# Three quarters of the MLPs' and of the second layer's inputs, and eight heads' probabilities, are turned in 32x32 blocks through DRAM instead of on TensorE

## The chip, the cores and the metric

The kernel runs on one core of one Trainium2 chip. The metric is the time of one execution on the device in microseconds. The kernel before took 2045.74 us (median of three runs, 2043.22 to 2048.05). The execution that was profiled took 2041.28 us, of which 2039.5 us are the span from its first to its last instruction.

## The reference

A two-layer encoder on 256 tokens of width 2048, all in float32. Each layer normalizes its input, projects it, runs twelve heads of its own kind and four heads into a memory of 256 tokens, projects the heads' outputs back (`w_o`), and runs an MLP with a squared ReLU. Layer 0's heads see a neighbourhood with a bias, layer 1's are grouped-query heads with normalized and rotated queries and keys.

```python
for i in range(DEPTH):
    n = rms_norm(h, attn_norm[i])
    ...
    h = h + jnp.concatenate([mix, cross], axis=-1) @ w_o[i]
    n = rms_norm(h, mlp_norm[i])
    h = h + jnp.square(jax.nn.relu(n @ w_up[i])) @ w_down[i]
return rms_norm(h, final_norm)
```

and a head of either kind is

```python
s = jnp.einsum(..., q, k) * scale (+ bias)
p = jax.nn.softmax(s, axis=-1)
return jnp.einsum(..., p, v)
```

## The kernel before, in words

**Products.** Every float32 operand is split in two parts of lower precision, `hi` and `lo` (`split`, L304: ScalarE copies to `hi`, VectorE subtracts for `lo`), and a product is three matmuls: hi by hi, hi by lo, lo by hi. Weights come from DRAM in chunks of 1 MB (`raw`, three buffers, loaded on SyncE's queue) and are split in halves; four pairs of halves are in hand. A half of an ordinary chunk is 12 matmuls of 512 columns.

**Turning.** The residual `h` lies with tokens on partitions. A projection needs its input with features on partitions, so it has to be turned: `transposed` (L318) has TensorE transpose 128x128 pieces into PSUM (`pt_n`), and `split_pair` (L329) takes them from there, times the norm's gain, into the two parts of `hT` (an MLP's input) or `nT` (a layer's input). The 2048 features are four column blocks of 512; a block is 8 transposes and 4 split pairs. A head's probabilities `sc` are turned too before they meet the values: by four transposes into `pt_a` (`attend2`, L406), or, in layer 0's twelve own heads, by the other way that the kernel has: VectorE transposes 32x32 blocks within their partitions (`turned`, L390), and `moved` (L352) puts the blocks in their places by writing them to DRAM in four pieces on SyncE's queue (`turn`) and reading them back in one on GpSimd's. `attend2_turned` then splits from there.

**Order.** `run_all` walks a list of grains (half chunks). A grain is a tick. `later(n, fn)` runs `fn` n ticks on, and loads and splits are written some grains ahead of their matmuls. A scheduler then orders each engine's instructions; on the chip each engine and each queue runs its own in order.

**Output projection and MLP input** (`o_done`, L646). When a column block `nb` of the projection is done, it is added to `h` and its squares are summed. The MLP's norm is one factor per token. Since a squared ReLU only scales, any positive factor will do for the input, if the result is corrected (`inv`, L671). Before, the factor came from the first three blocks (`guard`, ticks after the third), and only then were these three scaled (`scaled`) and transposed. The last block is prepared in `begun`, finished from PSUM and transposed on TensorE.

**Layer 1's input.** `down_done` (L986) closes a block of layer 0's MLP and has it transposed one tick later.

**Attention.** `attention` (L430) spreads a head's three steps (scores and softmax; turn; values) over ticks, `blocks` giving the distances for heads turned through DRAM. Layer 1's heads come four at a time (`b_q_done`, L1103), each four behind a block of queries.

Of the kernel before, what the change touches and what calls it, by code (L numbers as in the profile page):

```python
# [17 lines left out]
P = 128  # L18
D = 2048
# [20 lines left out]
GUARD = 3  # L40
# [38 lines left out]
def encoder_kernel(ctx: ExitStack, tc: tile.TileContext, t: dict, out: bass.AP):  # L79
# [70 lines left out]
    def halves_of(w):  # L150
# [9 lines left out]
        def prep(hf):  # L160
            if hf == 0:
                tiles["raw"] = at.ring.tile([P, CH], F32, tag="raw", bufs=3, name="raw")
                nc.sync.dma_start(tiles["raw"], w.src)
            tiles[hf] = new_half(w.kind)
            split(*tiles[hf], tiles["raw"][:, hf * HALF : (hf + 1) * HALF])
# [393 lines left out]
    def x_stats():  # L559
        ss = small.tile([P, NT], F32, tag="ss0", name="x_ss")  # L560
        for i in range(NT):
            for b in range(4):
                sq = at.work.tile([P, 512], F32, tag="b_y2", name="sq")
                nc.scalar.activation(sq, h[:, i, b * 512 : (b + 1) * 512], AF.Square, accum_out=ssq[0][:, i, b : b + 1])
        nc.vector.tensor_reduce(ss, ssq[0], axis=AX.X, op=ALU.add)
        box["x_col"] = keep.tile([P, NT], F32, name="x_col")
        nc.vector.tensor_copy(box["x_col"], rstd_of(ss, D, "x"))
        box["x_row"] = at.work.tile([P, SEQ], F32, tag="x_row", bufs=1, name="x_row")
        along_free(box["x_col"], box["x_row"])
# [75 lines left out]

    def o_done(layer, nb):  # L646
        which = 2 * layer

        def guard():

            box["near"] = mean_square(which, GUARD, "near")
            box["scale"] = keep.tile([P, NT], F32, tag="scale", name="scale")
            nc.gpsimd.tensor_tensor(box["scale"], box["near"], mhalf[:, :NT], op=ALU.pow)
            box["hT"] = wide(f"hT{layer}")

        def begun():

            y = at.side.tile([P, NT, 512], F32, tag="T", bufs=2, name="h_s")
            for i in range(NT):
                nc.scalar.activation(y[:, i, :], h[:, i, D - 512 :], AF.Copy, scale=box["scale"][:, i : i + 1])  # L660
            box["begun"] = y

        def scaled(b):
            y = at.side.tile([P, NT, 512], F32, tag="T", bufs=2, name="h_s")
# [3 lines left out]
            transposed(box["hT"], lambda i, k: y[:, i, k % 4 * P : (k % 4 + 1) * P],  # L668
                       list(range(b * 4, b * 4 + 4)), (G_M0, G_M1)[layer])
# [10 lines left out]
        def f(w):  # L680
            if nb == 0:
                closed("work")
                at.side = opened("side", side="right")
            def add():
# [8 lines left out]
            if nb < 3:  # L693
                add()
                squares()
            if nb == GUARD - 1:
                later(1, guard)
                for b in range(GUARD):
                    later(2 + 2 * b, scaled, b)
                later(7, begun)  # L700
# [210 lines left out]
    def plain_grains(layer, nb):  # L911
# [9 lines left out]
        def prep(c, hf):  # L921
            if c == 0:
                own[c, hf] = half_of_side(own[0], hf, PLAIN_AT)
            else:
                own[c, hf] = tuple(at.mlp.tile([P, HALF], F32R, tag="bt"[hf] + x, name=f"{x}_p") for x in "hl")
                split(*own[c, hf], own[1][:, hf * HALF : (hf + 1) * HALF])
# [58 lines left out]

    def down_done(layer, nb):  # L986
        def f(w):
# [7 lines left out]
            if nb == 0:  # L995
                box["nT"] = wide("nT1", 480)
            later(1, transposed, box["nT"], lambda i, k: h[:, i, k * P : (k + 1) * P],
                  list(range(nb * 4, nb * 4 + 4)), G_A1)
            if nb == 3:
# [3 lines left out]
                def norm():  # L1003
                    box["rstd"] = keep.tile([P, NT], F32, name="rstd1")
                    v = mean_square(1, 4, "full")
                    nc.gpsimd.tensor_tensor(box["rstd"], v, mhalf[:, :NT], op=ALU.pow)
# [96 lines left out]
    def b_q_done(blk):  # L1103
        def f(w):
# [5 lines left out]
                       for j, kv in enumerate(kvs)], 1, 2, 3)  # L1110
# [20 lines left out]
    def to_work():  # L1131
        closed("side")
        open_work(3)
# [144 lines left out]
```

## Time and profile before

| | before |
|---|---|
| median of the runs, us | 2045.74 (2043.22 to 2048.05) |
| the profiled execution, us | 2041.28 |
| its span, us | 2039.5 |
| VectorE, ScalarE, GpSimd, busy share of the span | 82%, 61%, 6% |
| DMA, mean over the span | 216 GB/s |
| weight chunks of 1 MB for the MLPs' first half | 128, 6.4 us from issue to landing |

In the groups below a row has the source line, the engine, the operation, what it writes and reads, the shapes and the count; then the busy time in us, the mean of one in ns, and the idle time of its engine just before with what ended it. Rows of the timeline have start and length in us first. Rows of windows have the stretch, its length and each engine's busy time with its number of instructions (TensorE's matmuls, its weight loads, VectorE, ScalarE, GpSimd), then TensorE's granted clock, the DMA share and GB/s. Rows of waits have the total, the number and the longest.

### The profile page before, as it was taken

The numbers are of one execution on the slowest core, as the hardware profiler recorded it, in microseconds if no ns is written. First come the engines' busy times: TensorE is split into PE (matmuls) and PEld (weight loads), VectorE is DVE, ScalarE is ACT, GpSimd is POOL, SyncE is SP. The second block draws the span as 40 slices with busy tenths as digits, with TensorE's granted clock in tenths as the row PEclk, the third lists the DMA queues.
The fourth block names the chain that finished last, engine by engine and source line by source line (L and its number), as shares of the span: only waits on it lengthen the run. The fifth ranks groups of instructions, "written<-read, shape, count | busy, mean of one in ns | idle before, by whom it ended". The sixth has DMA issues, their size and how long they took to land.

```text
span 2039.5 us, 32742 instructions
## 1 busy us (share of the span) xinstructions
PE 2018.9 (99%) x13044; PEld 1827.2 (90%) x13044; DVE 1665.5 (82%) x2049; ACT 1241.9 (61%) x1628; POOL 125.3 (6%) x156
## 2 busy tenths in 40 slices
PE   8999999999999999999999999999999999999998
PEld 7899999889999999999988888889999999999986
DVE  6767677558989999989997667657999999999896
ACT  6655455456666666666656557556666666666654
POOL 0000000000000000010000001000000000000000
PEclk9999999999999999999999999999999999999999
DMA  7756666727778787777765454537777787777773
GB/s 281 276 200 202 218 211 213 287 83 239 231 220 240 222 239 229 224 236 232 229 207 220 176 170 145 199 113 235 236 230 231 222 239 228 231 224 230 230 220 137
DMA packets 101306, 440.16 MB, mean 216 GB/s; under 512 B 11424, under 2 KB 19232, under 8 KB 68000
## 3 DMA queue, kind: packets, MB, share of 16 engines
q1 hardware_dynamic: 82800, 402.40, 58.4%
q0 software_dynamic: 17776, 34.61, 9.1%
q8 instruction: 102, 1.67, 0.3%
q10 hardware_dynamic: 576, 1.05, 0.1%
q14 instruction: 52, 0.43, 0.1%
HBM read 401.32 MB, written 7.34 MB: 200 GB/s over the span
## 4 chain that ended last, share of the span: by engine, by line
PE 95%; DVE 2%; DMA 1%; issue 1%; ACT 1%; SPq 0%; POOLq 0%; POOL 0%; DVEq 0%; ACTq 0%
PE ps_u L742 11%; PE ps_u L740 11%; PE ps_u L741 11%; PE p L859 9%; PE p L858 9%; PE p L857 8%; PE ps_m L214 8%; PE ps_m L217 8%; PE ps_m L218 8%; PE ps_s L226 3%; PE ps_s L228 3%; PE ps_s L227 3%; DVE ul L307 1%; DMA raw<-in_w_km 1%; PE pt_n L324 1%
## 5 line engine op out<-in xcount | busy, mean ns | idle before, releaser
L742 PE MATMUL ps_u<-hT,ul 128*128 128x256 f32 x2048 | 567.1, 277 | 2.3 <-DVE ul L307 2.3
L740 PE MATMUL ps_u<-hT,uh 128*128 128x256 f32 x2048 | 565.6, 276 | 0.1
L741 PE MATMUL ps_u<-hT,uh 128*128 128x256 f32 x2048 | 565.6, 276 | 0.0
L306 ACT ACTIVATE uh<-raw_U 128x1024 fp32r<-128x1024 f32 x278 | 294.6, 1060 | 306.6 <-PE ps_u L741 280.2
L740 PEld LDWEIGHTS ps_u<-hT,uh 128*128 128x128 f32 x2048 | 384.5, 188 | 5.7 <-ACT uh L306 0.5
L741 PEld LDWEIGHTS ps_u<-hT,uh 128*128 128x128 f32 x2048 | 384.3, 188 | 5.4
L742 PEld LDWEIGHTS ps_u<-hT,ul 128*128 128x128 f32 x2048 | 384.4, 188 | 4.5 <-DVE ul L307 3.5
L307 DVE TENSOR_TENSOR lo<-raw,hi 128x1024 fp32r<-128x1024 f32 (+1 forms) x224 | 266.1, 1194 | 148.8 <-ACT hi L306 147.4
L307 DVE TENSOR_TENSOR ul<-raw_U,uh 128x1024 fp32r<-128x1024 f32 x278 | 337.2, 1218 | 38.9 <-ACT uh L306 38.8
L306 ACT ACTIVATE hi<-raw 128x1024 fp32r<-128x1024 f32 (+1 forms) x224 | 231.5, 1039 | 205.4 <-PE ps_m L218 112.2
L306 ACT ACTIVATE th<-t 128x2048 fp32r<-128x2048 f32 x112 | 215.1, 1921 | 124.4 <-PE p L859 116.1
L307 DVE TENSOR_TENSOR tl<-t,th 128x2048 fp32r<-128x2048 f32 x112 | 256.1, 2287 | 29.9 <-ACT th L306 29.4
L307 DVE TENSOR_TENSOR bl<-b,bh 128x1536 fp32r<-128x1536 f32 x112 | 196.0, 1750 | 0.3
L858 PE MATMUL p<-tl,a_s 128*128 128x512 f32 x448 | 176.1, 393 | 0.3 <-DVE tl L307 0.3
L859 PE MATMUL p<-th,a_s 128*128 128x512 f32 x448 | 176.3, 394 | 0.0
L306 ACT ACTIVATE bh<-b 128x1536 fp32r<-128x1536 f32 x112 | 166.2, 1484 | 7.7 <-PE p L859 1.3
L837 POOL DMA_DIRECT2D t<-b x112 | 96.4, 860 | 1157.1 <-DVE t L836 551.8
L857 PE MATMUL p<-th,a_s 128*128 128x512 f32 x448 | 163.6, 390 | 0.0
L859 PE MATMUL p<-bh,a_s 128*128 128x512 f32 x336 | 131.7, 392 | 0.0
L858 PE MATMUL p<-bl,a_s 128*128 128x512 f32 x336 | 131.0, 390 | 0.0
L228 PE MATMUL ps_s<-nT,lo 128*128 128x256 f32 x448 | 125.4, 280 | 0.0
L226 PE MATMUL ps_s<-nT,hi 128*128 128x256 f32 x448 | 125.2, 279 | 0.0
(237 smaller groups left out, 3770.2 us busy)
## 6 DMA issues: line engine op xcount, KB each, us to landing
raw_U<-in_w_up SPq DMA_DIRECT2D x128, 1024.0 KB, 6.4
b<-in_w_pair SPq DMA_DIRECT2D x112, 768.0 KB, 4.5
raw<-in_w_o SPq DMA_DIRECT2D x32, 1024.0 KB, 5.0
t<-in_w_pair SPq DMA_DIRECT2D x112, 256.0 KB, 3.4
t<-b POOLq DMA_DIRECT2D x112, 256.0 KB, 6.7
raw<-in_w_b SPq DMA_DIRECT2D x21, 1024.0 KB, 5.0
raw<-in_w_av SPq DMA_DIRECT2D x12, 1024.0 KB, 5.0
raw<-in_w_aq SPq DMA_DIRECT2D x12, 1024.0 KB, 4.9
```

The source lines that it names most:

```text
L214: first = nc.tensor.matmul(w.ps[i], ah, hi[:, s], start=st, stop=False)
L217: nc.tensor.matmul(w.ps[i], ah, lo[:, s], start=False, stop=False)
L226: nc.tensor.matmul(ps, hi[:, s], acts[:, k, :SEQ], start=k == 0, stop=False)
L228: nc.tensor.matmul(ps, lo[:, s], acts[:, k, :SEQ], start=False, stop=k == KT - 1)
L306: first = nc.scalar.activation(dst_hi, src, AF.Copy)
L307: return first, nc.vector.tensor_tensor(dst_lo, src, dst_hi.bitcast(F32), op=ALU.subtract)
L740: nc.tensor.matmul(ps, hi[:, s], acts[:, k, :SEQ], start=k == 0, stop=False)
L741: nc.tensor.matmul(ps, hi[:, s], acts[:, k, SEQ:], start=False, stop=False)
L742: nc.tensor.matmul(ps, lo[:, s], acts[:, k, :SEQ], start=False, stop=k == KT - 1)
L857: nc.tensor.matmul(ps, a[:, 0, ai, :], hi[:, s], start=begins, stop=False)
L858: nc.tensor.matmul(ps, a[:, 0, ai, :], lo[:, s], start=False, stop=False)
L859: nc.tensor.matmul(ps, a[:, 1, ai, :], hi[:, s], start=False, stop=ends)
```

## The change

Two new functions carry it. `turned_rows` turns a column block as `turned` turns a head: 32x32 blocks on VectorE, then `moved`. `landed` splits what came back, times the gain, from SBUF: four ScalarE instructions and eight smaller VectorE ones for a block. `landed_past` places it behind the last weight split written so far.

- Both MLPs' inputs: the factor is now one known before the projection (layer 0: `x_col` of the kernel's input, layer 1: `rstd` of its own input), with its mean square kept for `inv`. So blocks 0 to 2 are scaled and turned each as it is done (`turning`), landing 6, 6 and 5 ticks later. Block 3 stays on TensorE.
- Layer 1's input: blocks 0 to 2 go the same way (`turned_input`), block 3 stays.
- Layer 1's first eight heads use `blocks=(0, 6, 8)`; the last four and the memory heads stay. The buffers for scores go from 3 to 7, and GpSimd's descriptor space in SBUF is set to 8192 bytes.

```diff
+    def turned_rows(src, room, back):
+        nc.vector.transpose(room.rearrange("p (b k i j) -> p i k b j", b=4, k=4, i=2),
+                            src.rearrange("p i (k b r) -> p i k b r", k=4, b=4))
+        back = back.rearrange("p (a f) -> p a f", a=4)
+        moved(back, room.rearrange("p (b f) -> p b f", b=4))
+        return back
+
+    def landed(dst, back, b, which):
+        src = back.rearrange("p a (k i j) -> p k i a j", k=4, i=2)
+        for k in range(4):
+            n, g = b * 4 + k, gain(which, b * 4 + k)
+            hi, lo = (dst[:, n, x * SEQ : (x + 1) * SEQ].rearrange("p (i a j) -> p i a j", i=2, a=4) for x in range(2))
+            nc.scalar.activation(hi, src[:, k], AF.Copy, scale=g)
+            for i in range(NT):
+                nc.vector.scalar_tensor_tensor(lo[:, i], src[:, k, i], g, hi[:, i].bitcast(F32),
+                                               op0=ALU.mult, op1=ALU.subtract)
+
+    def landed_past(*args):
+        past(lambda: landed(*args), box["splits"][-1])
...
-        def guard():
-            box["near"] = mean_square(which, GUARD, "near")
-            box["scale"] = keep.tile([P, NT], F32, tag="scale", name="scale")
-            nc.gpsimd.tensor_tensor(box["scale"], box["near"], mhalf[:, :NT], op=ALU.pow)
+        def factors():
+            box["scale"] = box[("x_col", "rstd")[layer]]
+            box["near"] = box[("x_mean", "mean")[layer]]
             box["hT"] = wide(f"hT{layer}")
...
+        def turning():
+            y = at.side.tile([P, 2, NT, 512], F32, tag="T", bufs=2, name="h_s")
+            scaled(y[:, 0], nb)
+            x, room = (y[:, n].rearrange("p a b -> p (a b)") for n in range(2))
+            back = turned_rows(y[:, 0], room, x)
+            later(LANDED[nb], landed_past, box["hT"], back, nb, (G_M0, G_M1)[layer])
...
             if nb < 3:
                 add()
+                turning()
                 squares()
-            if nb == GUARD - 1:
-                later(1, guard)
-                for b in range(GUARD):
-                    later(2 + 2 * b, scaled, b)
-                later(7, begun)
+            if nb == 2:
+                later(3, begun)
...
+    def turned_input(nb):
+        x, y = (at.side.tile([P, 3 * 512], F32, tag="b", bufs=2, name=n)[:, : 2 * 512] for n in ("h_t", "h_b"))
+        back = turned_rows(h[:, :, nb * 512 : (nb + 1) * 512], x, y)
+        later(6, landed_past, box["nT"], back, nb, G_A1)
...
-            later(1, transposed, box["nT"], lambda i, k: h[:, i, k * P : (k + 1) * P],
-                  list(range(nb * 4, nb * 4 + 4)), G_A1)
+            if nb < TURNED:
+                later(1, turned_input, nb)
+            else:
+                later(1, transposed, box["nT"], lambda i, k: h[:, i, k * P : (k + 1) * P],
+                      list(range(nb * 4, nb * 4 + 4)), G_A1)
...
-                       for j, kv in enumerate(kvs)], 1, 2, 3)
+                       for j, kv in enumerate(kvs)], 1, 2, 3, blocks=(0, 6, 8) if blk < 2 else None)
...
-        open_work(3)
+        open_work(7)
...
-    nc = _bacc.Bacc("TRN2", target_bir_lowering=False, num_devices=1)
+    nc = _bacc.Bacc("TRN2", target_bir_lowering=False, num_devices=1, dynamic_dma_scratch_size=8192)
```

Three places show how it moves instructions. Rows have the line, the operation, what is written and read, and the shape of what is written.

VectorE before, at layer 1's output projection, from the addition of the third column block (`h<-ps_m,h`) to the end of the MLP's input; `lo` and `ul` are splits of weights, `hT` are the small parts of the MLP's input, taken from TensorE's transposes:

```order
L687 TENSOR_TENSOR h<-ps_m,h 128x512 x2
L307 TENSOR_TENSOR lo<-raw,hi 128x1024
L635 TENSOR_REDUCE ss_t<-ssq_116 128x2
L637 TENSOR_SCALAR near<-ss_t 128x2
L307 TENSOR_TENSOR lo<-raw,hi 128x1024 x3
L333 SCALAR_TENSOR_TENSOR hT_13493<-pt_n,gains,hT_13493 128x256 x6
L307 TENSOR_TENSOR lo<-raw,hi 128x1024
L333 SCALAR_TENSOR_TENSOR hT_13493<-pt_n,gains,hT_13493 128x256 x6
L704 SCALAR_TENSOR_TENSOR h_s<-ps_m,scale,h_s 128x512 x2
```

Here the factor (`near`) and all splits of the input come after that addition, spread among the weight splits.

VectorE at the same place in the changed kernel, where the first row is again that addition:

```order
L716 TENSOR_TENSOR h<-ps_m,h 128x512 x2
L309 TENSOR_TENSOR lo<-raw,hi 128x1024 x5
L666 SCALAR_TENSOR_TENSOR hT_13341<-h_s,gains,hT_13341 128x128 x16
L309 TENSOR_TENSOR lo<-raw,hi 128x1024
L652 STREAM_TRANSPOSE h_s<-h_s 128x2x4x4x32
L731 SCALAR_TENSOR_TENSOR h_s<-ps_m,rstd_11393,h_s 128x512 x2
L666 SCALAR_TENSOR_TENSOR hT_13341<-h_s,gains,hT_13341 128x128 x8
L309 TENSOR_TENSOR ul<-raw_U,uh 128x1024
L335 SCALAR_TENSOR_TENSOR hT_13341<-pt_n,gains,hT_13341 128x256 x4
```

Blocks one and two (the row of 16) are split only after five weight splits, and the third block's transpose stands behind them, just ahead of the scaling of the fourth block out of PSUM.

VectorE in the changed kernel at layer 0's output projection, from the second half of the same addition (before, this place read like the first of these lists):

```order
L716 TENSOR_TENSOR h<-ps_m,h 128x512
L309 TENSOR_TENSOR lo<-raw,hi 128x1024
L666 SCALAR_TENSOR_TENSOR hT_4189<-h_s,gains,hT_4189 128x128 x8
L652 STREAM_TRANSPOSE h_s<-h_s 128x2x4x4x32
L309 TENSOR_TENSOR lo<-raw,hi 128x1024 x4
L666 SCALAR_TENSOR_TENSOR hT_4189<-h_s,gains,hT_4189 128x128 x8
L731 SCALAR_TENSOR_TENSOR h_s<-ps_m,x_col,h_s 128x512 x2
```

Here the third block's transpose has moved ahead, with four weight splits between it and its landing.

GpSimd's queue in the changed kernel at layer 1's first two blocks of queries, where before the reads `sc<-turn` were not there; `b_r_r` are the factors of the heads' norms, which ScalarE applies:

```order
L317 TENSOR_TENSOR b_r_r<-b_r_v,mhalf 128x4
L361 DMA sc<-turn 128x512
L1112 TENSOR_SCALAR b_r_r<-b_r_r,rstd_11393 128x4
L361 DMA sc<-turn 128x512 x3
L317 TENSOR_TENSOR b_r_r<-b_r_v,mhalf 128x4
```

The second half of one factor now stands behind the first head's read, which waits for its writes.

More of the change, by code (lines that the diff above doesn't have):

```diff
@@ L39 @@
 STEPS = PK // 2
-GUARD = 3
+TURNED = 3
+LANDED = 6, 6, 5
 MOVING_AT = 160
@@ L164, in prep @@
             tiles[hf] = new_half(w.kind)
-            split(*tiles[hf], tiles["raw"][:, hf * HALF : (hf + 1) * HALF])
+            box.setdefault("splits", []).append(split(*tiles[hf], tiles["raw"][:, hf * HALF : (hf + 1) * HALF]))
         def run(hf):
@@ L566, in x_stats @@
         box["x_col"] = keep.tile([P, NT], F32, name="x_col")
-        nc.vector.tensor_copy(box["x_col"], rstd_of(ss, D, "x"))
+        box["x_mean"] = keep.tile([P, NT], F32, name="x_mean")
+        nc.vector.tensor_scalar(box["x_mean"], ss, 1.0 / D, EPS, op0=ALU.mult, op1=ALU.add)
+        nc.gpsimd.tensor_tensor(box["x_col"], box["x_mean"], mhalf[:, :NT], op=ALU.pow)
         box["x_row"] = at.work.tile([P, SEQ], F32, tag="x_row", bufs=1, name="x_row")
@@ L644, in past, with scaled @@
             fn()
+    def turned_rows(src, room, back):
[15 more added lines that the diff above has]
+        past(lambda: landed(*args), box["splits"][-1])
     def o_done(layer, nb):
         which = 2 * layer
-        def guard():
-            box["near"] = mean_square(which, GUARD, "near")
-            box["scale"] = keep.tile([P, NT], F32, tag="scale", name="scale")
-            nc.gpsimd.tensor_tensor(box["scale"], box["near"], mhalf[:, :NT], op=ALU.pow)
+        def factors():
+            box["scale"] = box[("x_col", "rstd")[layer]]
+            box["near"] = box[("x_mean", "mean")[layer]]
             box["hT"] = wide(f"hT{layer}")
[L656 to L664, printed above, removed]
+        def scaled(y, b):
             for i in range(NT):
@@ L667, in scaled, with begun @@
                                      scale=box["scale"][:, i : i + 1])
-            transposed(box["hT"], lambda i, k: y[:, i, k % 4 * P : (k % 4 + 1) * P],
-                       list(range(b * 4, b * 4 + 4)), (G_M0, G_M1)[layer])
+        def begun():
+            box["begun"] = at.side.tile([P, NT, 512], F32, tag="T", bufs=2, name="h_s")
+            scaled(box["begun"], 3)
+        def turning():
[4 more added lines that the diff above has]
+            later(LANDED[nb], landed_past, box["hT"], back, nb, (G_M0, G_M1)[layer])
         def inv():
@@ L683, in f @@
                 at.side = opened("side", side="right")
+                factors()
             def add():
@@ L925, in prep @@
                 own[c, hf] = tuple(at.mlp.tile([P, HALF], F32R, tag="bt"[hf] + x, name=f"{x}_p") for x in "hl")
-                split(*own[c, hf], own[1][:, hf * HALF : (hf + 1) * HALF])
+                box["splits"].append(split(*own[c, hf], own[1][:, hf * HALF : (hf + 1) * HALF]))
         PIECES = ((0, 0, 0, 2), (0, 1, 2, 2), (1, 0, 4, 2), (1, 1, 6, 2))
@@ L1004, in norm @@
                     box["rstd"] = keep.tile([P, NT], F32, name="rstd1")
-                    v = mean_square(1, 4, "full")
-                    nc.gpsimd.tensor_tensor(box["rstd"], v, mhalf[:, :NT], op=ALU.pow)
+                    box["mean"] = mean_square(1, 4, "mean")
+                    nc.gpsimd.tensor_tensor(box["rstd"], box["mean"], mhalf[:, :NT], op=ALU.pow)
                 later(2, norm)
```

## The prediction, made before the changed kernel ran

> **What bounds the kernel now.** I read the page's busy line first, then its chain, then the list of TensorE's waits, then the two groups of transposes, and last the timeline around them.
>
> ```profile
> PE 2018.9 (99%) x13044; PEld 1827.2 (90%) x13044; DVE 1665.5 (82%) x2049; ACT 1241.9 (61%) x1628; POOL 125.3 (6%) x156
> PE 95%; DVE 2%; DMA 1%; issue 1%; ACT 1%; SPq 0%; POOLq 0%; POOL 0%; DVEq 0%; ACTq 0%
> PE ps_s L226 <- ACT hi L306: 6.7, 3, 6.1
> PE ps_u L742 <- DVE ul L307: 2.3, 5, 0.8
> PE av L419 <- ACT pT L306: 1.0, 1, 1.0
> ```
>
> TensorE is busy for 99% of the span and makes 95% of the chain; its longest wait (6.7 us) is in the start-up, and the rest is a few microseconds. So a TensorE instruction that goes is worth its place in TensorE's row, and whatever is added elsewhere costs nothing until TensorE has to wait for it. The question has two halves: what a transpose is worth, and which of the new waits reach TensorE.
>
> ```profile
> L324 PE MATMUL pt_n<-ident,h_s 128*128 128x128 f32 x64 | 8.6, 272 | 0.0
> L411 PE MATMUL pt_a<-ident,sc 128*128 128x128 f32 x80 | 12.9, 272 | 0.0
> 422.61 1.69 PE L324 MATMUL pt_n<-ident,h_s 128*128 128x128 f32 x14
> 424.05 0.47 PE L217 MATMUL ps_m<-lo,cat 128*128 128x512 f32 x1
> 424.37 0.39 PE L218 MATMUL ps_m<-hi,cat 128*128 128x512 f32 x1
> 424.59 0.39 PE L214 MATMUL ps_m<-hi,cat 128*128 128x512 f32 x1
> ```
>
> Each record is 272 ns long, but matmuls overlap: 64 records of 272 ns would be 17.4 us and the group is busy for 8.6. From the start of a run of 14 (422.61) to the next matmul's start (424.05) are 1.44 us, 103 ns for each. The step after a run is 0.32 us (424.05 to 424.37) where the ordinary step of a 512-column matmul is 0.22, so a run costs another 0.1 us. Spread over runs of four to fourteen that makes about **110 ns for a transpose**.
>
> The Trainium skill, "TensorE: Matmul & The Clock Gate", Part 4, gives about 275 ns for a transpose within a kernel; the record's 272 ns agrees as a length. If that were also what one occupies, the 104 that go would be worth 28.6 us; it is kept as a rival below.
>
> **The change part by part.**
>
> *Removed from TensorE.* Three of four column blocks of each MLP's input: 2 layers x 3 blocks x 8 = 48 transposes; three of four blocks of layer 1's input: 24; eight heads of layer 1 at 4 each: 32. Together 104, at 0.110 us: **-11.4 us** (2.6 + 2.6 + 2.6 + 3.5).
>
> *Added beside it.*
>
> ```profile
> L393 DVE STREAM_TRANSPOSE sc_t<-sc 128x512 f32<-128x512 f32 x12 | 8.5, 708 | 0.2
> L333 DVE SCALAR_TENSOR_TENSOR hT<-pt_n,gains,hT 128x256 fp32r<-128x256 f32 x32 | 14.1, 479 | 10.0 <-ACT hT L332 9.7
> L307 DVE TENSOR_TENSOR cat<-av,cat 128x128 fp32r<-128x128 f32 x24 | 6.9, 286 | 3.0 <-ACT cat L306 3.0
> L332 ACT ACTIVATE hT<-pt_n,gains 128x256 fp32r<-128x256 f32 x32 | 13.8, 476 | 10.2 <-PE pt_n L324 8.1 <-DVE hT L333 1.9
> 365.00:438.00 73.00, 73.00 (x339) 60.85 (x338) 41.35 (x50) 39.56 (x59) 0.71 (x1) 1.00 0.54 202
> 1045.00:1104.00 59.00, 59.00 (x307) 50.11 (x307) 47.58 (x58) 32.37 (x49) 0.00 (x0) 1.00 0.48 165
> 1127.00:1317.00 190.00, 189.03 (x975) 160.64 (x974) 128.37 (x231) 111.85 (x260) 15.01 (x16) 1.00 0.46 159
> 1317.00:1364.00 47.00, 46.90 (x219) 38.80 (x218) 28.95 (x37) 29.82 (x48) 0.73 (x1) 1.00 0.48 188
> ```
>
> The windows are, in order, layer 0's output projection, the end of its MLP, layer 1's projections with attention, and its output projection; behind TensorE's loads stand VectorE's, ScalarE's and GpSimd's busy time. For each of the nine blocks VectorE gets a block transpose of 1024 columns (estimated as two of 708 ns) and eight small splits instead of four of 479 ns. Eight at about 286 ns are 2.3 us against 1.9, so +1.8 us a block. Each of eight heads adds 0.7 us of transpose and 0.16 for its output split in halves. That is 23 us of VectorE, where these four windows leave it 123 us idle. ScalarE's splits stay as many (four of 476 ns). The traffic is 9 x 2 x 512 KB and 8 x 2 x 256 KB, 13 MB in windows whose DMA share is about 0.5. SyncE issues 9 x 4 + 8 x 4 = 68 more writes and GpSimd 17 more reads, each in order among the weight loads and row factors there. None of this reaches TensorE by its amount; the cover goes only where such a queue waits for a late transfer.
>
> The factor known early removes a small reduction on VectorE and a power on GpSimd in each layer, off TensorE's path: 0. I also price the smaller GpSimd descriptor space at 0: only the 112 accumulating loads use GpSimd much, and TensorE waits for none of them now. If it did stall them, they have the next rows' slack, so between 0 and +2.
>
> *The round trip.* Layer 0's heads already go this way, so the trace has its price:
>
> ```profile
> 174.13 0.71 DVE L393 STREAM_TRANSPOSE sc_t<-sc 128x512 f32<-128x512 f32 x1
> 184.07 0.63 ACT L306 ACTIVATE pT<-sc 128x512 fp32r<-128x512 f32 x1
> turn<-sc_t SPq DMA_DIRECT2D x48, 64.0 KB, 1.8
> sc<-turn POOLq DMA_DIRECT2D x12, 256.0 KB, 4.2
> mem_v<-vm_w SPq DMA_DIRECT2D x2, 512.0 KB, 6.4
> ACT pT L306 <- DMA sc<-turn: 10.9, 7, 3.3
> 200.00:400.00 200.00, 200.00 (x1312) 183.26 (x1311) 137.47 (x199) 102.25 (x167) 5.47 (x10) 1.00 0.68 232
> ```
>
> From the end of a head's block transpose (174.84) to its use (184.07) are 9.2 us. ScalarE waited for such data 10.9 us in all over seven of twelve heads, 3.3 at most, and still TensorE stayed busy for the whole window. That is the best evidence for the change: the same mechanism already runs without TensorE noticing.
>
> *Where it is late, 1: layer 1's MLP input.* In the new order VectorE does five splits after the third block is added, then sixteen small splits of blocks one and two, one more split, the third block's transpose, the fourth block's scaling, and then the third block's eight small splits. The third block cannot start sooner, since it needs a buffer of the first. In the old clock:
>
> ```profile
> 1339.34 1.28 DVE L687 TENSOR_TENSOR h<-ps_m,h 128x512 f32<-128x512 f32 x2
> 1349.08 1.23 DVE L307 TENSOR_TENSOR lo<-raw,hi 128x1024 fp32r<-128x1024 f32 x1 [0.81 <-ACT hi L306]
> 1364.08 0.28 PE L740 MATMUL ps_u<-hT,uh 128*128 128x256 f32 x1
> 1364.20 0.28 PE L741 MATMUL ps_u<-hT,uh 128*128 128x256 f32 x1
> ```
>
> The fifth split after the addition (1339.34) is the one at 1349.08, done at 1350.3. Sixteen small splits at 0.286 end at 1354.9, a split of 1.2 at 1356.1, a transpose of 1.4 at 1357.5. With the round trip of 9.2 the block is there at 1366.7, and with one ScalarE and two VectorE halves (0.5 + 0.6) usable at 1367.8. TensorE reaches its MLP 24 transposes earlier, at 1364.08 - 2.64 = 1361.4, has 24 matmuls on blocks one and two (0.113 to 0.12 us each, 2.7) and eight transposes (0.9), and stands at 1365.0. The wait is 2.8 us; at both ends of what the landings may be (a second leg 1.5 us shorter, or 512 KB taking 6.4 us instead of 4.2) 1.3 to 5.0. I take **+3.0**: this block of the saving is given back.
>
> The Trainium skill, "DMA: Bandwidth & Descriptors", section on the software path, fits a DMA as about 2.0 us plus bytes over 436 GB/s, 3.2 us for 512 KB; this case's 256 KB read takes 4.2 where the fit gives 2.6. With the fit for both legs the wait would come out near 1 us, and the sum 2 us lower.
>
> *Late, 2: the eight heads.*
>
> ```profile
> L1073 ACT ACTIVATE b_y<-ps_m,rstd 128x128 f32<-128x128 f32 x32 | 11.3, 387 | 2.3 <-PE ps_m L218 2.3
> L1073 ACT ACTIVATION_READ_ACCUMULATOR b_y<-ps_m,rstd 128x1 f32 x32 | 7.2, 227 | 0.0
> L307 DVE TENSOR_TENSOR pT<-sc,pT 128x512 fp32r<-128x512 f32 x12 | 8.3, 689 | 5.3 <-ACT pT L306 5.3
> ```
>
> From the start of four heads' scores (24 matmuls of 0.12 us and one other, 3.1) TensorE has 70 matmuls of 0.227 us (15.9) before the first head's product with the values: 19.0. In VectorE's new order that head's transpose stands behind a small operation on the next queries' sums of squares; those wait for four of the 70 matmuls (0.9) and take ScalarE 4 x 0.61 = 2.5. So 3.1 + 0.9 + 2.5 = 6.5, a transpose 0.7, the round trip 9.2, and the split on ScalarE and VectorE 0.6 + 0.7: 17.7. That is 1.3 us to spare, and later heads have more. With the longest wait above (3.3) two blocks' first heads lose 2 us each; I take **+1.0** of 0 to +4, nearer 0 because layer 0 showed none.
>
> *Late, 3: the other two inputs.*
>
> ```profile
> 413.02 1.28 DVE L687 TENSOR_TENSOR h<-ps_m,h 128x512 f32<-128x512 f32 x2
> 437.76 0.28 PE L740 MATMUL ps_u<-hT,uh 128*128 128x256 f32 x1
> 1093.71 1.40 DVE L880 SCALAR_TENSOR_TENSOR h<-ps_m,inv,h 128x512 f32<-128x512 f32 x2
> 1105.81 0.39 PE L214 MATMUL ps_m<-uh,nT 128*128 128x512 f32 x1
> ```
>
> In layer 0 the order is kinder: after the third block's addition come two splits (2.4) and eight small ones (2.3), then its transpose (1.4): 413.0 + 1.3 + 6.1 = 420.4, usable 9.2 + 1.1 later, 430.7; TensorE wants it at 437.8 - 2.6 + 2.7 = 437.9. For layer 1's input: 1093.7 + 1.4, a split and a transpose give 1097.7, usable at 1108; TensorE wants it some 72 matmuls after 1105.8 - 2.6, at 1119.5, though ScalarE now has four weight splits ahead of it that need their own loads. **+0.5** together, of 0 to +2.
>
> *Sum:* -11.4 + 3.0 + 1.0 + 0.5 = **-6.9 us**. The profiled execution took 2041.3 us (span 2039.5 and 1.8 around it), so 2034.4. It is 4.4 below the median of the runs, 2045.7, and on that scale the forecast is **2038.8**. A measurement tells about 0.2%, 4.1 us, from no change.
>
> **The rivals.**
>
> *All hidden.* The landings are quicker than layer 0's, and nothing waits: -11.4 us, 2034.3. For it: layer 0's heads. Against it: the third block of layer 1 has no slack on paper.
>
> *Given back.* The long ends hold: 5 us at layer 1's MLP, 3 in the heads, 1 elsewhere: -11.4 + 9.0 = -2.4 us, 2043.3, not to be told from no change.
>
> *Slower.* GpSimd's row has the first head's read ahead of the row factor of the second block of queries; that factor waits for the head's write to land, ScalarE's next work waits for the factor, and the weight splits stand behind it. The read's landing spread bears on it:
>
> ```profile
> DMA to landing us min/median/max: 1.7/2.4/5.7
> ```
>
> If every head's leg took the longest landing there, 5.7 rather than 2.4 us (3.3 more), and the reserve of split weights took only 0.9 of it, TensorE would wait 8 x 2.4 = 19 us: with the 3.5 of the two other places -11.4 + 19.2 + 3.5 = +11.3, 2057. It decides from (11.4 - 3.5) / 8 = 1.0 us a head. Against it: in layer 0 the same reads stand in the same queue, and TensorE ran through.
>
> *Full length.* Transposes occupy their 272 ns: -28.3 + 4.5, 2021.9. The starts above speak against it.
>
> That the change leaves the transposes where they were is out: the new order of TensorE lacks them.
>
> **How the numbers follow.** Forecast 0.48, all hidden 0.20, given back 0.19, slower 0.11, full length 0.02. The forecast's own bounds are 2036 to 2043; the range goes from a little below all hidden to a little above given back, **2032 to 2046**, and leaves out the slower case, full length and some tails. Faster by over 0.2% (below 2041.6): 0.43 of the forecast, all of all hidden, full length and a little of given back, 0.67. Within 0.2%: 0.22. Slower: 0.11.
>
> **What would show it.** TensorE's transposes should fall from 64 to 16 (of h_s), from 32 to 8 (of h) and from 80 to 48 (of sc). In layer 1's first MLP matmuls a wait of TensorE for hT's third block, some 3 us, confirms that step; none refutes it. A wait of the value products for pT shows the heads' share. The split groups (hi, lo) should show no new wait for GpSimd or DMA. The prediction is wrong if TensorE's waits outside these places grow, or if the landing of turned data is far from 9 us.

## The result and the profile after

| | before | after |
|---|---|---|
| median of 7 runs, us | 2043.22 (2040.9 to 2050.87) | 2033.99 (2028.57 to 2039.0) |
| ratio after to before | | 0.9944, 95% interval 0.9929 to 0.9959 |
| the profiled execution, us | 2041.28 | 2035.79 |
| its span, us | 2039.5 | 2034.0 |

The change makes the kernel faster: by medians 9.2 us, by the ratio 11.4 (8.4 to 14.5). The forecast was 2038.8, a gain of 6.9. The two profiled executions differ by only 5.5. These numbers disagree by more than some of the terms that were forecast, so the first question is which of them the change made.

The page of the changed kernel has the busy line and the chain; below them stand the transposes in the list of all its groups, and TensorE's list of waits:

```profile
PE 2009.7 (99%) x12940; PEld 1815.3 (89%) x12940; DVE 1680.8 (83%) x2105; ACT 1241.3 (61%) x1636; POOL 134.0 (7%) x171
PE 91%; DVE 4%; DMA 2%; issue 1%; ACT 1%; SPq 0%; POOLq 0%; POOL 0%; DVEq 0%; ACTq 0%
L326 PE MATMUL pt_n<-ident,h_s 128*128 128x128 f32 x16 | 2.4, 272 | 0.0
L326 PE MATMUL pt_n<-ident,h 128*128 128x128 f32 x8 | 1.2, 272 | 0.0
L413 PE MATMUL pt_a<-ident,sc 128*128 128x128 f32 x48 | 7.6, 272 | 0.0
```

```profile
PE ps_s L228 <- ACT hi L308: 6.6, 1, 6.6
PE ps_u L769 <- DVE ul L309: 2.8, 6, 0.8
PE ps_m L216 <- ACT cat L308: 1.6, 2, 1.3
PE p L885 <- DVE tl L309: 1.4, 2, 1.2
PE ps_s L230 <- DVE lo L309: 0.8, 1, 0.8
PE ps_m L220 <- DVE cat L309: 0.7, 1, 0.7
PE ps_s L228 <- DVE km_s L350: 0.6, 1, 0.6
PE ps_u L768 <- DVE hT L666: 0.3, 1, 0.3
PE ps_u L767 <- ACT hT L664: 0.2, 1, 0.2
```

TensorE has 104 instructions less, as the change says: its transposes fell from 64 to 16 (of `h_s`), from 32 to 8 (of `h`) and from 80 to 48 (of `sc`). Two waits are new and belong to it: `cat` (1.6 and 0.7, at layer 1's output projection) and `hT` (0.3 and 0.2, at the first products of layer 1's MLP). The wait of a head's values for `pT` (1.0 before) is gone. The wait for `tl` is in the middle of an MLP, where nothing was changed.

These waits are the profile's own count, from the modelled end of one matmul to the next one's start. A stricter account takes the starts alone: the step from one matmul's start to the next, less the ordinary step (0.227 us for 512 columns, 0.1135 for 256). So the three steps at `cat` in

```profile
1279.25 0.40 PE L220 MATMUL ps_m<-hi,cat 128*128 128x512 f32 x1
1280.96 0.50 PE L216 MATMUL ps_m<-hi,cat 128*128 128x512 f32 x1 [1.32 <-ACT cat L308]
```

and behind it lose 1.5 + 0.9 + 0.5 = 2.8 us, and those at `hT` 0.4 + 0.5 + 0.6 = 1.5 (the last one for a weight part, `ul`, that VectorE splits right behind). The same starts cut the kernel into stages. Each number below is the time from the start of one matmul to that of another, in one profiled execution; the second execution of each kernel is told of in the first experiment.

| stage, us | before | again | after | again |
|---|---|---|---|---|
| start, to layer 0's first projection | 95.2 | 93.6 | 94.0 | 93.4 |
| layer 0's projections and heads | 244.5 | 244.5 | 244.5 | 244.5 |
| A: layer 0's output projection to its MLP's 300th product | 128.5 | 129.5 | 125.7 | 125.7 |
| the middle of layer 0's MLP | 585.3 | 591.7 | 585.2 | 585.3 |
| B: the MLP's last part, in which layer 1's input is turned | 46.3 | 46.3 | 43.5 | 43.5 |
| C: layer 1's projections and heads to its MLP's 300th product | 294.7 | 294.7 | 292.4 | 293.1 |
| the middle of layer 1's MLP | 586.4 | 587.8 | 589.9 | 585.8 |
| the last part of layer 1's MLP | 43.3 | 43.3 | 43.3 | 43.3 |

The change can work only in A, B and C. The other stages hold the same instructions on TensorE in both kernels, and still the middles of the MLPs move by 6 us between two executions of one kernel.

### The profile page after: what moved, and what is told of

The parts are those of the page before. It is cut to its first block, busy times and chain, and to the rows that moved or that the text cites. A ratio compares the mean times of both kernels' runs of the same rounds, so it can differ in the third digit from the quotient of the medians.

```text
span 2034.0 us, 32804 instructions
## 1 busy us (share of the span) xinstructions
PE 2009.7 (99%) x12940; PEld 1815.3 (89%) x12940; DVE 1680.8 (83%) x2105; ACT 1241.3 (61%) x1636; POOL 134.0 (7%) x171
## 4 chain that ended last, share of the span: by engine, by line
PE 91%; DVE 4%; DMA 2%; issue 1%; ACT 1%; SPq 0%; POOLq 0%; POOL 0%; DVEq 0%; ACTq 0%
PE ps_u L769 11%; PE ps_u L768 10%; PE ps_u L767 10%; PE p L886 8%; PE p L885 8%; PE p L884 8%; PE ps_m L216 8%; PE ps_m L219 8%; PE ps_m L220 8%; PE ps_s L230 3%; PE ps_s L228 3%; PE ps_s L229 3%; DVE ul L309 1%; DMA raw<-in_w_km 1%; DMA t<-in_w_pair 1%
## 5 line engine op out<-in xcount | busy, mean ns | idle before, releaser
L309 DVE TENSOR_TENSOR tl<-t,th 128x2048 fp32r<-128x2048 f32 x112 | 256.1, 2287 | 17.1 <-ACT th L308 16.6
L863 DVE TENSOR_TENSOR t<-t,b 128x512 f32<-128x512 f32 x112 | 77.3, 690 | 69.1 <-DMA t<-in_w_pair 50.0
```

The lines of the kernel that those rows point to most:

```text
L309: return first, nc.vector.tensor_tensor(dst_lo, src, dst_hi.bitcast(F32), op=ALU.subtract)
```

## The experiments

### The same two kernels again

Both kernels were profiled a second time, unaltered.

> The changed kernel unaltered, for a second profiled execution and a tighter ratio. In the first one TensorE's steps beyond the ordinary step of each matmul add up to 5.0 us more than before (34.9 against 29.9), of which 2.8 stand at layer 1's output projection behind cat (before: 1.1 at a head's values), 1.5 at the first MLP products of layer 1, 1.3 at one expert-like product p<-tl, 0.5 at the start. Theory P (the price per transpose was right, the waits vary from one execution to the next): ratio again 0.993 to 0.996; the waits behind cat and hT return within 1 us, since their order is fixed, and the 1.3 at p<-tl and the start do not return. Rival Q (the gain comes from somewhere else too, and the profiled execution merely lacks it): the waits return as they were, span again 2034 +-1, and the ratio is near 0.9970.

> The kernel before, unaltered, for a second profiled execution. By stages the changed kernel's two profiled executions are 7.4 to 7.6 us shorter than before where the change works (layer 0's projection to its MLP's first products -2.8, layer 1's input -2.8, layer 1's attention to its MLP's first products -1.7 to -2.3), while the medians differ by 9.2 both times. Theory R (the rest is late weights in the stages that the change doesn't touch: the start and the middle of the MLPs, which differ from execution to execution): the three stages repeat within 0.3 us (128.5, 46.3, 294.7), and start plus the middles of the MLPs (95.2, 585.3, 586.4 in the first) move by 1 to 4 us. Rival V (the change gives more in its own stages than the first pair of executions shows): one of the three stages is 1 us or more longer than in the first execution.

The changed kernel took 2032.38 us (five runs) against 2041.58, ratio 0.9952 (0.9938 to 0.9967); the kernel before against itself came out at 1.0006 (0.9995 to 1.0017), though its two sets of runs have medians of 2045.50 (twelve) and 2042.87 (seventeen). In its second execution the changed kernel's waits were

```profile
PE ps_m L216 <- ACT cat L308: 1.7, 2, 1.4
PE ps_m L220 <- DVE cat L309: 0.7, 1, 0.7
PE ps_u L768 <- DVE hT L666: 0.3, 1, 0.3
PE ps_u L767 <- ACT hT L664: 0.2, 1, 0.2
```

while the one for `tl` is not in the list. In the second one of before it was 3.2 us, in five places, where it had been 0.3:

```profile
PE p L858 <- DVE tl L307: 3.2, 5, 1.4
```

So the waits behind `cat` and `hT` come with the order of the instructions and return to a tenth, as theory P said; those for `tl` come and go. In the table A, B and C sum to 469.5 and 470.5 before and 461.7 and 462.3 after: **the change gives 7.2 to 8.9 us in its own stages, 8.0 between the means**. That is theory R's answer in the main, with two misses: the start and the middles of the MLPs moved by 6.2 us (1 to 4 expected), and A was 1.0 us longer the second time (0.3 expected), just where rival V begins.

The 1.0 us of A is not a wait. From the 100th to the 300th product of that MLP the starts are 22.67 us apart in the first execution (451.67 to 474.34) and 23.55 in the second (451.03 to 474.58): TensorE goes from one product to the next in 118 ns instead of 113, with the granted clock at 1.00 in both. The same slower step is in the first part of layer 1's MLP in the second execution of the changed kernel (23.29 us against 22.77). It comes in kernels with and without the change, and its cause is open. Without it A, B and C are 7.9 us shorter with the change, so rival V doesn't hold. The rest of the 9.2, and what the ratio adds, fits within what the other stages do between two executions; a cause that ties it to the change was not found.

### What a transpose is worth

Every transpose of `pt_n` and `pt_a` is made twice, in the kernel before: 64 + 32 + 80 = 176 more.

```diff
-                nc.tensor.transpose(pt[:, k, ...], sc[:, s, ...], ident)
+                for _ in range(2):
+                    nc.tensor.transpose(pt[:, k, ...], sc[:, s, ...], ident)
```

> The kernel before with every transpose of pt_n and of pt_a made twice, 176 more. At the forecast's 0.110 us each: +18 to +19.5 us, ratio 1.009. At the length of their record, 272 ns: +48 us, ratio 1.023. If layer 0's and layer 1's transposes lay in time that TensorE loses anyway: under 10 us.

2062.81 us against 2041.58, ratio 1.0107 (1.0089 to 1.0125): 21.2 us, which would be 0.12 us for a transpose, a little more than the 18 to 19.5 us expected. But the medians also hold what the other stages do. The stages in which the doubled transposes lie (layer 0's heads, A, B and C) take 733.1 us against 714.0 and 715.0 in the two executions before, 18.2 to 19.2 more: **0.10 to 0.11 us for a transpose**. Stage B of the changed kernel, with 24 transposes less, is 2.80 us shorter, 0.117 each. The forecast's 0.110 lies between the two, which fits its working of 103 ns for each and 0.1 us for a run: doubling adds no run, and a block that goes takes its runs along. The rival that had them occupy the 272 ns of their record falls. With it falls what the Trainium skill's "TensorE: Matmul & The Clock Gate", Part 4, would have given if its 275 ns were what one occupies (28.6 us for the 104).

### The parts that were priced at nothing

The kernel before with the MLP's early factor and the descriptor space of 8192 bytes, and nothing else of the change.

```diff
-            box["near"] = mean_square(which, GUARD, "near")
...
+            box["scale"] = box[("x_col", "rstd")[layer]]
+            box["near"] = box[("x_mean", "mean")[layer]]
...
+    nc = _bacc.Bacc("TRN2", ..., dynamic_dma_scratch_size=8192)
```

> The kernel before with only the parts that the forecast priced at 0: the MLP's factor from the earlier sums (layer 0: the kernel's input, layer 1: its own input) and the smaller descriptor space; all transposes stay on TensorE. Theory P: no difference, ratio 0.999 to 1.001, and TensorE's steps add up as before outside the start and the p<-tl waits. Rival: if these give the part of the gain beyond the forecast (some 2 us), the ratio is 0.999 or less.

2043.64 us, ratio 1.0005 (0.9997 to 1.0014): nothing, as forecast. In its profiled execution A, B and C sum to 471.3, 0.8 to 1.8 us above before, and 1.3 of that is the slower step of the products told of above.

### Inputs and heads apart

One kernel turns layer 1's heads on TensorE again, and one has them alone.

```diff
-    ... 1, 2, 3, blocks=(0, 6, 8) if blk < 2 else None)
+    ... 1, 2, 3)
```

> The changed kernel with layer 1's eight heads turned on TensorE again, the inputs still through DRAM. Theory P: 32 transposes return (+3.5 us), the wait behind cat at layer 1's output projection goes (-2.8, with some 1 us at a head's values back): +1 to +2 us against the changed kernel, ratio to before about 0.9955. The forecast's terms would have given +2.5. Rival 'all hidden' (the heads wait for nothing in most executions): +3.5, ratio 0.996.

> The kernel before with only the eight heads turned through DRAM (with the larger score pool and the smaller descriptor space that it needs). Theory P: -3.5 us of transposes, +1.5 to +2.8 of waiting behind cat at the output projection: -0.7 to -2 us, ratio 0.999 to 0.9997. 'All hidden': -3.5 us, ratio 0.998. If the descriptor space or the pool were a gain of its own: over 4 us, below 0.998.

With the heads back: 2031.0 us, ratio 0.9945 (0.9933 to 0.9958). The heads alone: 2038.87, ratio 0.9986 (0.9975 to 0.9997). The first was expected to be 1 to 2 us slower than the changed kernel (2032.38 beside it) and was 1.4 faster. By stages: A and B as in the changed kernel, and C at 291.9, so that C is shorter with 24 transposes gone than with 56 gone (292.4, 293.1). Alone they shorten C by 1.5 us, to 293.2. **The eight heads, 32 transposes worth 3.3 to 3.7 us, bring nothing where the inputs are turned too.** Without them the waits for `cat` and for `hT` are both gone from TensorE's list.

### Why the heads bring nothing

The place is the seventh of the eight heads. SyncE's, GpSimd's and ScalarE's rows in the changed kernel's timeline around it, with start, length, engine, line and, in brackets, the idle time before and what ended it (SPq and POOL rows are DMAs being issued):

```profile
1261.56 4.57 SPq L165 DMA_DIRECT2D raw<-in_w_o  x2
1266.60 6.57 SPq L360 DMA_DIRECT2D turn<-sc_t  x8
1274.18 0.54 POOL L361 DMA_DIRECT2D sc<-turn  x1 [10.27 <-DMA turn<-sc_t]
1275.56 0.54 POOL L361 DMA_DIRECT2D sc<-turn  x1 [0.84 <-DVE lo L309]
1279.17 0.63 ACT L308 ACTIVATE pT<-sc 128x512 fp32r<-128x512 f32 x1 [5.80 <-DMA sc<-turn]
1280.66 0.26 ACT L308 ACTIVATE cat<-av 128x128 fp32r<-128x128 f32 x1
```

The time from issue to landing is in the answers on single tiles (least, median, most). For the sixth head's four writes, the weight load that was issued at 1265.8, and the seventh head's writes behind it:

```profile
DMA to landing us min/median/max: 1.7/1.8/1.8
DMA to landing us min/median/max: 7.1/7.1/7.1
DMA to landing us min/median/max: 5.1/6.0/6.5
```

64 KB that land in 1.8 us otherwise take 6 when they are issued 0.8 us behind a load of 1 MB. GpSimd's queue stands idle for 10.3 us until they are there, ScalarE for 5.8 us until the read has landed, and in ScalarE's queue the split of an earlier head's output (`cat`) stands behind the late `pT`. TensorE doesn't wait for the late head at all: it waits for `cat`. From the end of this head's block transpose (1266.57) to its use (1279.17) are 12.6 us, where the forecast had taken 9.2 for every head.

Four kernels test it. The first gives the eight heads' writes to GpSimd, the second those of the last two heads to ScalarE, the third those to GpSimd, and the fourth turns these two heads on TensorE. The edit of the first three is

```diff
-            nc.sync.dma_start(to[a], src[32 * a : 32 * a + 32])
+            (queue or nc.sync).dma_start(to[a], src[32 * a : 32 * a + 32])
...
+    res = turned(res, nc.gpsimd if blocks[2] == 8 else None)
```

(then `nc.scalar` and `nc.gpsimd` for `head in (6, 7)`), and for the fourth

```diff
+            n = (4, 2, 0)[blk]
+            if n:
+                attention(jobs[:n], 1, 2, 3, blocks=(0, 6, 8))
+            if n < 4:
+                attention(jobs[n:], 1 + 2 * n, 2, 3)
```

> The changed kernel, with the eight heads' four writes issued by GpSimd instead of SyncE; everything else, and each read, as it was. Theory W (the 2.9 us that TensorE loses behind cat come from the seventh head's four writes: SyncE issues them just behind a 1 MB weight load that takes 7.1 us, and they land 5.1 to 6.5 us after their issue instead of 1.8; ScalarE then waits 5.8 us for that head, with the split of cat queued behind): the writes no longer stand behind a weight load, the seventh head is there some 4 us sooner, the wait behind cat falls under 1 us, and the time by 2 to 3 us against the changed kernel. Rival S (the distance of 6 and 8 ticks is too short there, whatever queue writes): 2 to 3 us of waiting behind cat remain and the time stays within 1 us. Rival G (GpSimd's own queue becomes the late one): heads land later than before, and the time is 2 us or more above the changed kernel.

> The changed kernel, with the writes of only the seventh and eighth head issued on ScalarE's queue; all others stay on SyncE. Theory W: these eight writes no longer stand behind the weight load on SyncE, land in about 2 us (5.1 to 6.5 before), the seventh head's split waits under 2 us instead of 5.8, and the 2.9 us behind cat go: -2 to -3 us against the changed kernel, 2029 to 2031. Rival S (distance too short whatever the queue): the waits stay, 2032 to 2034. Rival T (the transfers share the 16 DMA engines with the weight load, so another queue doesn't help): the writes land in 4 us or more again.

> The changed kernel, with the writes of only the seventh and eighth head issued by GpSimd, which has nothing else in its queue there than the reads. Theory W: as with ScalarE's queue, -2 to -3 us against the changed kernel if GpSimd's writes land in 2 to 4 us. Theory G (an in-order queue shared by a head's read and the next head's write is the trouble, as in the run with all eight heads on GpSimd, 5.2 us at a head's values): one head is late again and the time is 2033 or above.

> The changed kernel with the second block's third and fourth head turned on TensorE again, so that six heads are left in DRAM: 8 transposes return (+0.9 us). Theory W: those two heads' writes are the ones behind two weight loads in a row, so the wait behind cat (2.9) goes, at most 1.1 us at a head's values comes back: 1 to 2 us faster than the changed kernel, about the time with all heads back (2031) or up to 1 below it. Rival S: another head is late in their place, 2 us or more of waiting behind cat stay, and the time is 1 us above the changed kernel's.

| kernel | median, us | ratio to before | stage C, us |
|---|---|---|---|
| all eight heads' writes on GpSimd | 2038.34 | 0.9980 (0.9971 to 0.9988) | 298.9 |
| the last two heads' on ScalarE | 2034.26 | 0.9956 (0.9944 to 0.9969) | 292.7 |
| the last two heads' on GpSimd | 2035.73 | 0.9965 (0.9952 to 0.9977) | 294.2 |
| the last two heads on TensorE | 2029.15 | 0.9933 (0.9922 to 0.9945) | 288.4 |

Of these four values of C, 0.9, 0.9, 0.9 and 0.6 us are the slower step of the MLP's products (0.1 in the changed kernel's 292.4).

*All on GpSimd* is rival G. TensorE's wait for a head's split shows it, and GpSimd's timeline of the same kernel shows why: it writes one head's four pieces and then must wait for the next heads' transposes before it reaches the first head's read. GpSimd's in-order queue was also what the forecast's slower rival feared, but there for a factor that stands behind a read, and here it is a read that stands behind writes.

```profile
PE av L421 <- ACT pT L308: 5.2, 1, 5.2
```

```profile
1263.34 2.28 POOL L360 DMA_DIRECT2D turn<-sc_t  x4 [12.82 <-DVE sc_t L395]
1266.77 1.63 POOL L360 DMA_DIRECT2D turn<-sc_t  x3 [1.16 <-DVE rs L387]
1268.71 0.55 POOL L360 DMA_DIRECT2D turn<-sc_t  x1 [0.30 <-issue]
1269.43 2.18 POOL L360 DMA_DIRECT2D turn<-sc_t  x4 [0.18 <-issue]
1271.60 0.57 POOL L361 DMA_DIRECT2D sc<-turn  x1
```

*Another queue for the last two* is a miss of theory W, and the landings are those of rival T. The landing of those eight writes, first on ScalarE's queue, then on GpSimd's:

```profile
DMA to landing us min/median/max: 1.6/4.4/5.4
```

```profile
DMA to landing us min/median/max: 3.1/4.7/6.0
```

The weight load beside them took 7.1 and 7.0 us again. The writes are no longer behind it in a queue and are still late, so their place in a queue is not what holds them. Start and time to landing together show more: in all three kernels the first of the late writes lands 0.2 us after the load, and the next ones follow at 0.2 us.

| writes issued by | the load landed at, us | the first late write landed at, us |
|---|---|---|
| SyncE (changed kernel) | 1272.85 | 1273.05 |
| ScalarE | 1272.53 | 1272.73 |
| GpSimd | 1272.63 | 1272.80 |

So the load holds them, whichever engine issues them. That this is because they share the DMA engines, as rival T has it, is argued; no run isolates it. The Trainium skill, "DMA: Bandwidth & Descriptors", section on queues, rings and completion order, has each engine serve its queues in turn, packet by packet; by that rule alone small writes on another queue need not wait for the whole load, and the landing times don't show it. The same section has the increment that tells of a landing come only after every earlier write of that engine, across its queues; the landing times agree with that, and no run here tests it by itself.

The wait for `cat` went, and others took its place: 0.4 and 0.9 us at other steps with ScalarE's queue, 1.9 at a head's values with GpSimd's, and the steps at `hT` grew from 1.5 to 1.9 and 2.4. With GpSimd's queue the sign of its theory G (one head late, 2033 or above) is met too. ScalarE's run, where reads and writes share no queue, has the late writes all the same.

*Without the last two heads* no head's writes are issued right behind a weight load: the nearest stand 3.0 us behind one and land in 1.8 to 2.2 us. None of the waits of TensorE for `cat`, `hT` or `pT` is left, and C falls to 288.4, 4.0 to 4.6 us below the changed kernel (1 to 2 were expected), although 8 transposes are back. The place of a head's writes among the weight loads decides, as theory W said; only the remedy by another queue was wrong.

### The second block of heads, and the late third column block

First the second block's four heads on TensorE, then layer 1's third column block (`by_pe` scales it and has it transposed as before):

```diff
-    blocks=(0, 6, 8) if blk < 2 else None)
+    blocks=(0, 6, 8) if blk < 1 else None)
```

```diff
-                turning()
+                if (layer, nb) == (1, 2):
+                    later(2, by_pe, nb)
+                else:
+                    turning()
...
-                later(3, begun)
+                later(4, begun)
```

> The changed kernel with the second block's four heads on TensorE again: 16 transposes return (+1.9 us). Theory W: no wait behind cat, no wait of hT; against the changed kernel -1 to -2.5, and 1.9 us below the kernel with all heads back if the first block's four are free: 2029. Rival S: the first block's heads cost a wait of their own, and it stands at 2031 or above.

> The changed kernel with the third block of layer 1's MLP input turned on TensorE again (8 transposes, +0.9 us), two ticks after its addition. The trace of the changed kernel shows 1.5 us of waiting at the MLP's first products (0.38, 0.54 and 0.57 above the ordinary steps), where the forecast had 3.0. If that is what this block costs: 0.6 us faster than the changed kernel, not to be told in the time, but the waits for hT are gone from TensorE's list. By the forecast's 3.0 it would be 2.1 faster. If the wait belongs to something else (it is absent where the eight heads are back on TensorE): it stays, and the time is 1 us longer.

Four heads through DRAM: 2029.81 us, ratio 0.9940 (0.9928 to 0.9952), C at 290.0. That is 4.7 us less than before for 24 + 16 = 40 transposes, 0.117 each: the first block's four heads are free.

The third column block on TensorE again: 2034.18 us, 0.9957 (0.9945 to 0.9969), C at 291.7, so 0.8 to 1.4 less than the changed kernel, with no wait for `hT`. The wait of 1.5 is that block's. Its transpose and its landing in VectorE's and ScalarE's timeline, in the changed kernel and then in the one with six heads:

```profile
1330.35 0.69 DVE L716 TENSOR_TENSOR h<-ps_m,h 128x512 f32<-128x512 f32 x1 [1.76 <-PE ps_m L220]
...
1342.11 4.29 DVE L666 SCALAR_TENSOR_TENSOR hT<-h_s,gains,hT 128x128 fp32r<-128x128 f32 x16
1347.45 1.23 DVE L652 STREAM_TRANSPOSE h_s<-h_s 128x1024 f32<-128x1024 f32 x1
1356.79 1.71 ACT L664 ACTIVATE hT<-h_s,gains 128x256 fp32r<-128x256 f32 x4 [8.97 <-DMA h_s<-turn]
```

```profile
1328.72 0.69 DVE L716 TENSOR_TENSOR h<-ps_m,h 128x512 f32<-128x512 f32 x1 [1.76 <-PE ps_m L220]
...
1340.38 1.23 DVE L652 STREAM_TRANSPOSE h_s<-h_s 128x1024 f32<-128x1024 f32 x1
1349.77 1.71 ACT L664 ACTIVATE hT<-h_s,gains 128x256 fp32r<-128x256 f32 x4 [6.93 <-DMA h_s<-turn]
```

In the changed kernel 17.1 us pass from the block's addition to its transpose, with six heads 11.7: VectorE gets to it 5.4 us sooner. From the end of the transpose to the landing it is 8.1 us in both. So the eight heads cost twice: 2.8 us at `cat`, and the order that comes with them makes the third block late by 1.5.

### More of what has slack

The kernel with six heads, and the four memory heads of a layer turned through DRAM as well; first layer 1's, then (without these) layer 0's.

```diff
-                   for j in range(NMH)], 1, 0, 0)
+                   for j in range(NMH)], 1, 1, 3, blocks=(0, 6, 8))
```

```diff
-            attention([(q, box["km"][:, hd, :], None, ..., box["cat"])], 1)
+            attention([(q, box["km"][:, hd, :], None, ..., box["cat"])], 1, blocks=(0, 4, 5))
```

> Six heads as in e6, and layer 1's four memory heads turned through DRAM too, which come first in the layer and are needed only at its end: 16 transposes less. If a transpose is worth 0.11 to 0.12 us wherever the turned data has slack: -1.8 us against e6, 2027 to 2028. If the reads on GpSimd or the writes behind weight loads make something else late: no gain or a wait of 1 to 3 us at layer 1's first heads.

> Six heads as in e6, and layer 0's four memory heads turned through DRAM too: 16 transposes less, -1.8 us against e6 if they have slack. They come in the projections' first part, where four score buffers are all that there is, two for each head on its way: if that is too few, ScalarE and VectorE wait for buffers and TensorE's stage of 244.45 us from the first projection to the output projection grows by 1 us or more.

Layer 1's: **2025.74 us, ratio 0.9908** (0.9893 to 0.9923), the best version here, some 17 us below the kernel before and with C at 286.0, 2.4 below the six heads alone. It lies a little below the 2027 to 2028 expected; of the 2.4, 0.6 is the slower step of the products in the run with six heads, and the 1.8 that is left is what was expected of 16 transposes. Layer 0's: 2031.05, ratio 0.9934 (0.9918 to 0.9950), nothing gained. Its stage of 244.5 us grew to 245.5 though it had lost 16 transposes, with a new wait of a head's values:

```profile
PE av L421 <- ACT pT L308: 1.9, 2, 1.7
```

That the four score buffers there are too few is the guess of the expectation; the run shows only that the turned heads are late.

## Why the prediction was off, step by step

*A transpose occupies 110 ns, 104 of them 11.4 us:* right in kind and in size. By stages, doubling gives 0.10 to 0.11 and stage B 0.117, so 10.7 to 12.2 us went.

*Nothing for VectorE's, the DMAs' and the queues' added work, the factor and the descriptor space:* right for the factor and the space (ratio 1.0005) and for layer 0. In A and B no wait appeared, so "late, 3" (+0.5) was 0: the stages lost 2.8 us each (A up to 3.8 with the slower step in one of its executions), where the forecast had 2.6 each, less 0.5 for both. For DMAs it was wrong at one place, as the heads show.

*Late, 1, the third block of layer 1, +3.0:* the mechanism was right, the size was half, +1.5. VectorE came to the transpose 17.1 us after the addition (16.8 in the forecast). Two lengths in its working failed. The round trip, 9.2 us taken from layer 0's heads, was 8.1 here, with a read of 512 KB that landed in 3.7 us and no weight load beside it; and TensorE, expected at the block 25.7 us after the addition (1339.34 to 1365.0), came after 26.6 (1330.35 to 1357.35, less the wait of 0.4). What the forecast did not see is that the lateness itself hung on the heads.

*Late, 2, the heads, +1.0 of 0 to +4:* net +1.7, in size within the range (2.8 behind `cat` less the 1.1 at a head's values that went), but that is luck, for the path was another. It was placed at the first head of each block and at the wait for `pT`; it came at the seventh head, through a weight load that held up its writes, and reached TensorE through ScalarE's queue as a wait for `cat`, a place that is not among those the prediction named. The round trip was treated as one length, while it depends on what is being loaded when the writes are issued: 12.6 us behind the load.

*The sum, -6.9, "on that scale the forecast is 2038.8":* A, B and C give -7.2 to -8.9, so the sum was 1.1 us short of their mean of -8.0. In C alone, forecast -2.1 (6.1 for 56 transposes, 4.0 given back), the trace has -1.7 to -2.3. The 11.4 of the forecast less what the traces show as given back (1.5 + 1.7 + 0) is 8.2: the mis-sized terms of the sum are the late ones, 3.2 together instead of 4.5, and the largest error is the third block of layer 1, 1.5 instead of 3.0.

**The step that failed most is the scale.** The sum was first set against the profiled execution (2034.4) and then moved up by 4.4 us to the median of three runs, 2045.74. The changed kernel's median was 2033.99 and its profiled execution took 2035.79. Before measured 2043.22 over the seven runs of the result and 2041.6 to 2043.2 in four later sets, with 2045.50 in a fifth, so a median of a few runs is good to some 2 us only, a third of the gain that was forecast. Against 2043.22 the number 2038.8 says -4.4, where 9.2 came. Of the 4.8 us by which 2038.8 missed 2033.99, 2.5 are the scale and 1.1 the sum; the remaining 1.2 stay open.

*The rivals:* "all hidden" at 2034.3 comes nearest to the measured time, and it is not what happened: waits of 2.8 and 1.5 us are in the trace both times. "Given back" and "slower" did not occur; a queue of GpSimd that holds up a head, as the slower one feared, did appear as soon as GpSimd also wrote.

## What to carry to other kernels

A block that is turned through DRAM is free where its landing has slack and worth nothing where it hasn't; so count the slack of each block by itself, and take those back that lack it. For this, look at which large load is under way when its small writes are issued (here another queue did not save them), and at what else stands in the queue of the engine that will wait for the data. With differences of a few us in 2000, sum up the stages that a change can reach and compare those between executions, and put a forecast on a base of many runs.

## What the runs showed of the hardware

A head's four writes of 64 KB each landed in 1.8 us with no load just ahead, and in 5.1 to 6.5 us when issued 0.8 us behind a 1 MB load on the same queue; on ScalarE's queue it was 4.4 in the median and on GpSimd's 4.7, beside the same load. From each of the three queues the first of them landed 0.2 us after the load. A 32x32 block transpose of 128x1024 took 1.23 us on VectorE, less than twice the 0.71 for 128x512. One kernel, with the granted clock the same, spent 585.3 and 591.7 us in the middle of an MLP, with waits for weight parts (`tl`) that come and go. And at a granted clock of 1.00, 200 products of 256 columns took 22.67 us in one execution and 23.55 in another of the same kernel, a step of 118 ns instead of 113.
